# RWKV-7 and pooling trunk on one core: the value turned by VectorE through DRAM, the key norm's reciprocal spread through DRAM, scalings, bonus and gate moved

## The chip, the cores and the metric

The kernel runs on one core of a Trainium2 chip. The metric is the device time of one execution in microseconds (us). The engines are called as the profile calls them: PE is TensorE (matmuls and transposes by matmul), DVE is VectorE, ACT is ScalarE, POOL is GpSimd, SP is SyncE, which here only issues DMAs; SPq and ACTq are the queues of DMAs that SP and ACT issue.

## What is computed

One layer of a decoder trunk on 512 tokens of width 2048, all in float32, then an RMSNorm. Cut to what matters here:

```python
z = rms_norm(x) @ W_in            # r, k, v, decay and rate inputs | gate | pool input | pool gate
zs = zs + (token_shift(zs) - zs) * mu
w = exp(-exp(-softplus(-(w0 + tanh(wd) @ w_up)) - 0.5)); a = sigmoid(a0 + ad @ a_up)
kk = k * k_k;  kk = kk / max(norm(kk over each head's 64 channels), 1e-12)
k = k * (1 + (a - 1) * k_a)
# per head (16 heads of 64), token after token:
S = S * w + (S @ -kk) (kk * a)^T + v k^T;   y = S @ r
y = head_group_norm(y) * ln_w + ln_b
y_rwkv = (y + sum(r * k * r_k) * v) * silu(g_rwkv)
# pool half: trailing means over 2, 4, 8, 16 tokens, a 256x256 map per group, times silu(gate)
x = x + concat(y_rwkv, y_pool) @ W_out
x = x + sigmoid(x @ W_pg + b_pg) * (p @ W_ple);   out = rms_norm(x) * final_g
```

## The kernel before

Everything lies with channels on the partitions and the 512 tokens along the free axis. Large products are made of three matmuls (`mm3`, L164): each operand is split into a rounded high part and the rest, and high by high, high by low and low by high are summed in PSUM. A weight chunk (128 rows by 512, or four 128x128 tiles side by side) is loaded raw by a DMA on SP, cast to its high part by ACT (L132), and its low part is a subtraction on DVE (L133). The pool of chunks has four buffers of each kind, so chunk n takes the buffers of chunk n-4: its raw load waits for the subtraction of chunk n-4 on DVE, and its cast for the last matmul that uses chunk n-4. The raw loads are queued on SP in the order of the chunks, among SP's other DMAs. Engines execute in order, and the order on each engine is fixed when the program is built: a scheduler places the instructions, except that the order of PE's matmuls is held as the program issues them (`keep_in_program_order`, L156), and that `tc.issue_after(i)` keeps an instruction behind instruction i.

The 16 heads are worked in eight blocks j of two heads (128 channels). A block goes through these functions:

- `prepare_key` (L554): kk is the square of the scaled key (ACT), split into high `kqh` (ACT) and low `kql` (DVE, L138).
- `norm_key` (L563): PE sums the squares of each head, `pss`; DVE evicts it with a maximum (L568). `scale_key` (L570): DVE's reciprocal over 128x512 (L572) and a product (L573). (The reciprocal is taken of the sum of squares; the root isn't needed, as kk enters twice.)
- `decay_and_rate` (L519): two small products `pu` and `pa`, the tile `sig` and its running sum, the decays `pw` and `ipw`, the rate `tha`.
- `prepare` (L577): on DVE the operands `ar` (L594, L597) and `bk` (L596, and its second half L600, which needs the scaled key kk and tha), and `kp`; SP stores bk to DRAM (L607).
- `scores` (L617): 32 matmuls `pm` from bk and ar, masked into `mt` on DVE (L632); `pbo` and the bonus `bv`; then mt's small blocks go through DRAM (nd, L648, and n, L653), and bk comes back as `bg` in pieces of 32x32x32 (L659) for two DVE block transposes into `bkn` (L614).
- `invert` (L664): 31 steps on DVE invert the small triangular blocks; the result goes through DRAM (xd, L679) into `x1` (L686), four reads on SP.
- `gather` (L692): the next block's `prepare_key` and `decay_and_rate`; the value `v_` is turned by four PE transposes into `pv` (L702) and copied by ACT into `uv` (L704, L705); the next block's `norm_key`; y1, two 32x256 block transposes of x1 on DVE (L729); 32 matmuls each `pq` (from y1), `pmv` and `px`. Then the pending `finish` of the block before.
- `recur` (L762): eight chunks of 64 tokens, one after the other: py, zs, pu, uv, ps and sbd go round PE, DVE and ACT. At its end the eight statistics of y and the eight scalings of `ysb` (L866).
- `finish` (L870): PE transposes ysb into `pyt` (L874), ACT adds the norm's bias, DVE adds the bonus and multiplies with the gate (L877, L878), and ACT's queue stores the result.

Each engine's share of this is filled with the large projections: `pump(n)` lets PE go on with n matmuls of the streams zk, zr, zv, zg and zb (the next block's key, receptance, value and gate, and a pooling unit's columns). The counts are constants (L517, L883), so PE's place in the stream at each step of a block is the same every time the program is built. In the loop at L901 a turn prepares block j+1 (`prepare`), runs the recurrence of block j with `scores(j+1)` and `invert(j+1)` woven in, and ends with `gather(j+1)`. After the eight blocks come the output product acc_o and the embedding gate acc_g, with weights streamed in the same way. The gather of block j is called gather(j) here: it works for block j and begins block j+1.

Of the kernel before, what the change touches and what calls it, by code (L numbers as in the profile page):

```python
# [34 lines left out]
def trunk_kernel(ctx: ExitStack, tc: tile.TileContext, x, p, norm_g, w_in, mu, w0, w_up, a0, a_up,  # L35
# [527 lines left out]
    def norm_key(j):  # L563
# [4 lines left out]
        late[0] = nc.vector.tensor_scalar(kk, ps, 1e-24, None, ALU.max)  # L568

    def scale_key(j):  # L570
        k_, kk = need("k", j), kks[j][0]
        nc.vector.reciprocal(kk, kk)  # L572
# [4 lines left out]
    def prepare(j):  # L577
# [22 lines left out]
        nc.vector.tensor_tensor(bk[:, :, 1:3, :], k4, i4, ALU.mult)  # L600
# [16 lines left out]
    def scores(j):  # L617
# [43 lines left out]
        st_[j].update(mt=mt, nb=nb, bv=bv, bg=bg)


    def invert(j):  # L664
# [18 lines left out]
        for par in range(2):  # L683
            pb = 64 * (1 - par)
            for b in range(2):
                nc.sync.dma_start(out=x1[pb + 32 * b:pb + 32 * b + 32, :, 32 * b:32 * b + 32],  # L686
                                  in_=xd[par, b].rearrange("u i q c -> (i q) u c"))
# [4 lines left out]
    def gather(j):  # L692
        d = st_[j]
        v_, mt = d.pop("v_"), d["mt"]
        if j + 1 < NJ:
# [32 lines left out]
        with tc.issue_after(late[0].ins):  # L728
            yt = [nc.vector.transpose(y1[pb:pb + 32], x1[pb:pb + 32, :, 0:32]) for pb in (0, 64)]  # L729
# [464 lines left out]
```

## Time and profile before

| | us |
|---|---|
| median of three runs | 1085.88 (1085.88, 1084.61, 1088.7) |
| the profiled execution | 1087.06 |
| its span | 1085.3 |
| busy: PE | 1057.8 |
| busy: DVE | 714.9 |
| busy: ACT | 441.3 |
| busy: POOL | 70.9 |
| mean granted clock of TensorE | 0.996 |

The profiled execution was 1.2 us above the median and 1.8 us longer than its span, which runs from the first to the last recorded instruction. The eight blocks take the first 720 us of the span or so, acc_o and acc_g the rest. A row of the timeline gives start and duration in us, engine, line, operation, output and inputs, the shape, and in brackets how long the engine had waited and for what. Durations on PE are those of the whole pipeline: the next matmul can start before the one ahead of it has ended, so PE's pace is read from one start to the next. On DVE, too, the next instruction starts some 0.07 us before the recorded end of the last.

### The profile page before, as it was taken

The page shows a single profiled execution, that of the slowest core. Times are in us where ns is not written, and L with a number is a line of the kernel's source. Part 1 is how long each engine was busy: PE and PEld are TensorE (multiplying, and loading weights), DVE is VectorE, ACT ScalarE, POOL GpSimd, SP SyncE. Part 2 cuts the span into 40 slices and gives each one's busy share as a digit, 9 for nine tenths or more (in the row PEclk, how much of TensorE's full clock was granted, in tenths as well). Part 3 has the DMA queues.
Part 4 walks back from the last instruction along what each step waited for, and adds up shares of the span by engine and source line. Part 5 has one row for each costly group of instructions (what it writes and reads, how often), then busy time and mean ns, then how long its engine had stood idle before and what let it go on. Part 6 is the DMA issues. An engine that isn't in the chain of part 4 may idle for free.

```text
span 1085.3 us, 17105 instructions
## 1 busy us (share of the span) xinstructions
PE 1057.8 (97%) x5996; PEld 873.7 (80%) x5996; DVE 714.9 (66%) x1851; ACT 441.3 (41%) x901; POOL 70.9 (7%) x180
## 2 busy tenths in 40 slices
PE   5999999999999999999999999999999999999996
PEld 4888878888888887887888788888888888888885
DVE  6676968878779779688887966464432424445366
ACT  7633535335336244353353344543222222333337
POOL 2100010010110100100101101000000000000000
PEclk9999999999999999999999999999999999999999
DMA  7444443442533533433435343774434428354534
GB/s 234 112 120 113 135 115 86 114 123 74 156 93 110 143 95 100 117 87 107 115 95 152 99 127 104 244 238 152 166 126 142 168 97 263 129 180 150 178 99 156
DMA packets 212916, 146.94 MB, mean 135 GB/s; under 512 B 68085, under 2 KB 173150, under 8 KB 212830
## 3 DMA queue, kind: packets, MB, share of 16 engines
q1 hardware_dynamic: 192126, 112.28, 35.9%
q10 hardware_dynamic: 20704, 33.56, 9.5%
q8 instruction: 47, 0.77, 0.3%
q14 instruction: 39, 0.32, 0.1%
HBM read 122.21 MB, written 23.07 MB: 134 GB/s over the span
## 4 chain that ended last, share of the span: by engine, by line
PE 76%; DVE 4%; DMA 1%; ACT 1%; issue 0%; SPq 0%; ACTq 0%; DVEq 0%
PE acc_o L157 16%; PE acc_g L157 16%; PE zb L157 13%; PE zg L157 5%; PE zv L157 5%; PE zr L157 5%; PE zk L157 4%; PE pple L157 2%; PE py L157 2%; PE pu L157 1%; PE pm L157 1%; DMA n<-nd 1%; PE pp L157 1%; PE ps L157 1%; PE pmv L157 1%; PE px L1015 1%
## 5 line engine op out<-in xcount | busy, mean ns | idle before, releaser
L133 DVE TENSOR_TENSOR wlo_g<-raw_g,whi_g 128x512 fp32r<-128x512 f32 x84 | 57.1, 685 | 76.0 <-ACT whi_g L132 76.0
L157 PE MATMUL zb<-hhi,whi_b 128*128 128x512 f32 x256 | 106.0, 414 | 0.0
L133 DVE TENSOR_TENSOR wlo_o<-raw_o,whi_o 128x512 fp32r<-128x512 f32 x64 | 43.9, 690 | 91.4 <-ACT whi_o L132 91.4
L157 PE MATMUL zb<-hhi,wlo_b 128*128 128x512 f32 x256 | 100.4, 392 | 0.0
L157 PE MATMUL acc_o<-whi_o,ylo 128*128 128x512 f32 x256 | 100.2, 391 | 0.0
L157 PE MATMUL acc_o<-whi_o,yhi 128*128 128x512 f32 x256 | 99.9, 390 | 0.0
L157 PE MATMUL zb<-hlo,whi_b 128*128 128x512 f32 x256 | 99.8, 390 | 0.0
L157 PE MATMUL acc_o<-wlo_o,yhi 128*128 128x512 f32 x256 | 99.7, 390 | 0.0
L132 ACT CAST whi_g<-raw_g 128x512 fp32r<-128x512 f32 x84 | 52.0, 621 | 106.4 <-PE acc_g L157 59.4
L157 PE MATMUL acc_g<-whi_g,x2hi 128*128 128x512 f32 x208 | 81.2, 391 | 0.0
L157 PE MATMUL acc_g<-wlo_g,x2hi 128*128 128x512 f32 x208 | 81.0, 389 | 0.0
L157 PE MATMUL acc_g<-whi_g,x2lo 128*128 128x512 f32 x208 | 80.6, 389 | 0.0
L132 ACT CAST whi_o<-raw_o 128x512 fp32r<-128x512 f32 x64 | 39.9, 623 | 97.0 <-PE acc_o L157 96.7
L827 POOL TENSOR_SCALAR s0p<-sbd,pw 64x64 f32<-64x64 f32 x96 | 54.5, 568 | 338.6 <-DVE sbd L820 251.0
L132 ACT CAST whi_b<-raw_b 128x512 fp32r<-128x512 f32 x64 | 39.7, 621 | 85.4 <-PE zb L157 28.8
L133 DVE TENSOR_TENSOR wlo_b<-raw_b,whi_b 128x512 fp32r<-128x512 f32 x64 | 43.7, 684 | 28.0 <-ACT whi_b L132 27.6
L157 PEld LDWEIGHTS zb<-hhi,wlo_b 128*128 128x128 f32 x256 | 48.0, 188 | 10.9
L675 DVE TENSOR_TENSOR xw<-xw,tm 128x60 f32<-128x60 f32 (+24 forms) x248 | 52.1, 210 | 7.0
L157 PEld LDWEIGHTS acc_o<-wlo_o,yhi 128*128 128x128 f32 x256 | 48.1, 188 | 10.0
L157 PEld LDWEIGHTS acc_o<-whi_o,ylo 128*128 128x128 f32 x256 | 48.1, 188 | 9.8
L157 PEld LDWEIGHTS acc_o<-whi_o,yhi 128*128 128x128 f32 x256 | 48.1, 188 | 9.7
L157 PEld LDWEIGHTS zb<-hhi,whi_b 128*128 128x128 f32 x256 | 48.2, 188 | 8.3
(283 smaller groups left out, 2532.0 us busy)
## 6 DMA issues: line engine op xcount, KB each, us to landing
raw_b<-in_w_in_dram SPq DMA_DIRECT2D x64, 256.0 KB
raw_o<-in_w_out_dram SPq DMA_DIRECT2D x64, 256.0 KB
raw_g<-in_w_pg_dram SPq DMA_DIRECT2D x64, 256.0 KB
raw_k<-in_w_in_dram SPq DMA_DIRECT2D x32, 256.0 KB
raw_r<-in_w_in_dram SPq DMA_DIRECT2D x32, 256.0 KB
raw_v<-in_w_in_dram SPq DMA_DIRECT2D x32, 256.0 KB
raw_g<-in_w_in_dram SPq DMA_DIRECT2D x32, 256.0 KB
bkd<-bk SPq DMA_DIRECT2D x8, 512.0 KB
```

The costliest lines, as they stand in the source:

```text
L132: nc.scalar.copy(hi, raw)
L133: nc.vector.tensor_tensor(lo, raw, hi.bitcast(F32), ALU.subtract)
L157: i = nc.tensor.matmul(*a, **k)
L675: nc.vector.tensor_tensor(xw[:, 0:n_, s + 1:32], xw[:, 0:n_, s + 1:32], tm[:, 0:n_, 0:w_], ALU.add)
L827: nc.gpsimd.tensor_scalar(s0p[hc, :], nxt[hc, hc], pcn[hc], None, ALU.mult)
L1015: nc.tensor.transpose(pt[:, tt * P:(tt + 1) * P], x2[tt][:, i * P:(i + 1) * P], ident)
```

## The change

It has four parts.

The value. The four PE transposes and two ACT copies go. In `prepare` SP stores `sv` to DRAM (vd, 256 KB, behind the last x1 read); after the n reads in `scores` four DMAs on SP fetch it back as `vg` in pieces of 32x16x32, and in `gather` two DVE block transposes of 64x512 make uv from it. vg takes one of the four buffers of the tag "t"; in `gather` the next block's sig takes that buffer again, so that ACT's write of sig waits for the two transposes.

The key's norm. `prepare_key(j+2)` and `norm_key(j+2)` are called at the fifth and sixth chunk of `recur(j)`; they were called in `gather(j+1)`. For all blocks but block 0, ACT evicts pss, one row of each head (2x512) goes to DRAM (nrd), comes back as 128x8 (nr), the maximum and the reciprocal run on 128x8, and the result goes to DRAM (ird) and comes back as kk in two broadcast reads of 64x512, all on SP. Block 1's key keeps its place in gather(0).

The scalings of ysb move from the end of `recur` into the next `gather`, behind the two y1 transposes. The bonus and the gate of `finish` (two DVE instructions, one DMA on ACT's queue) move into the next block's `prepare`, behind the second half of bk.

What stands on PE otherwise is the same sequence, with the 32 transposes pv gone and each pss of blocks 2 to 7 some chunks earlier. SP issues 75 DMAs more in all (607 for 532): five for each value, and five for each key's norm from block 1 on. In the first gather, gather(0), the rows on DVE around the y1 transposes were these (names carry the block's number: y10 is the y1 of block 0, kk1 the key of block 1):

```order
L133 TENSOR_TENSOR wlo_b0_1_1059<-raw_b0_1_1056,whi_b0_1_1058 128x512
L592 TENSOR_TENSOR kp1_1646<-kp1_1646,sk1_1280 128x512
L568 TENSOR_SCALAR kk1_1429<-pss1_1489 128x512
L729 STREAM_TRANSPOSE y10_1548<-x10_1150 32x256 x2
L572 RECIPROCAL kk1_1429<-kk1_1429 128x512
L133 TENSOR_TENSOR wlo_b0_2_1065<-raw_b0_2_1062,whi_b0_2_1064 128x512
L133 TENSOR_TENSOR wlo_b0_3_1159<-raw_b0_3_1156,whi_b0_3_1158 128x512
L370 SCALAR_TENSOR_TENSOR sv1_1523<-zv1_1383,prm_131,sv1_1523 128x511
```

and are now:

```order
L609 TENSOR_TENSOR kp1_1657<-kp1_1657,sk1_1287 128x512
L610 TENSOR_SCALAR tha1_1463<-tha1_1463 128x512
L611 TENSOR_TENSOR ar1_1655<-sr1_1387,pw1_1455 128x4x2x64
L613 TENSOR_TENSOR bk1_1656<-kp1_1657,ipw1_1456 128x4x2x64
L614 SCALAR_TENSOR_TENSOR ar1_1655<-sk1_1287,dprm_133,pw1_1455 128x4x128
L133 TENSOR_TENSOR wlo_b0_2_1072<-raw_b0_2_1069,whi_b0_2_1071 128x512
L526 TENSOR_TENSOR as2_1654<-ar2_1651,as2_1654 64x128
L758 STREAM_TRANSPOSE y10_1560<-x10_1157 32x256
L133 TENSOR_TENSOR wlo_b0_3_1166<-raw_b0_3_1163,whi_b0_3_1165 128x512
L370 SCALAR_TENSOR_TENSOR sv1_1535<-zv1_1390,prm_131,sv1_1535 128x511
L758 STREAM_TRANSPOSE y10_1560<-x10_1157 32x256
```

The second y10 transpose stands behind two products into ar, one into bk, two weight subtractions and the shift of the value sv1, and the reciprocal is gone. On SP, in the same gather, the reads of x10 stood here:

```order
L129 DMA raw_b0_2_1062<-in_w_in_dram 128x4x128
L679 DMA xd0_1145<-xw0_1080 256x1x32 x2
L129 DMA raw_b0_3_1156<-in_w_in_dram 128x4x128
L686 DMA x10_1150<-xd0_1145 32x8x32 x4
L129 DMA raw_g1_0_1162<-in_w_in_dram 128x4x128
L129 DMA raw_g1_1_1184<-in_w_in_dram 128x4x128
```

and stand here now:

```order
L129 DMA raw_b0_2_1069<-in_w_in_dram 128x4x128
L708 DMA xd0_1152<-xw0_1087 256x1x32 x4
L129 DMA raw_b0_3_1163<-in_w_in_dram 128x4x128
L129 DMA raw_g1_0_1169<-in_w_in_dram 128x4x128
L129 DMA raw_g1_1_1191<-in_w_in_dram 128x4x128
L715 DMA x10_1157<-xd0_1152 32x8x32 x4
L129 DMA raw_g1_2_1197<-in_w_in_dram 128x4x128
```

The weight loads g1_0 and g1_1 are ahead of x10's reads. A little later, ahead of block 1's pm, DVE had these rows up to the second half of bk (L600, in the changed kernel L617):

```order
L597 SCALAR_TENSOR_TENSOR ar1_1644<-sk1_1280,dprm_133,pw1_1448 128x4x128
L599 TENSOR_TENSOR kk1_1429<-kk1_1429,tha1_1456 128x512
L133 TENSOR_TENSOR wlo_g1_0_1165<-raw_g1_0_1162,whi_g1_0_1164 128x512
L600 TENSOR_TENSOR bk1_1645<-kk1_1429,ipw1_1449 128x4x128
L601 SCALAR_TENSOR_TENSOR kp1_1646<-sr1_1380,dprm_133,kp1_1646 128x512
L526 TENSOR_TENSOR as2_1643<-ar2_1640,as2_1643 64x128
L133 TENSOR_TENSOR wlo_g1_1_1187<-raw_g1_1_1184,whi_g1_1_1186 128x512
```

and has now:

```order
L133 TENSOR_TENSOR wlo_g1_1_1194<-raw_g1_1_1191,whi_g1_1_1193 128x512
L851 TENSOR_SCALAR sbd1_567<-ps0_0_1703,pw0_837 64x64 x2
L133 TENSOR_TENSOR wlo_g1_2_1200<-raw_g1_2_1197,whi_g1_2_1199 128x512
L590 SCALAR_TENSOR_TENSOR kk1_1436<-sk1_1287,prm_131,kk1_1436 128x512
L616 TENSOR_TENSOR kk1_1436<-kk1_1436,tha1_1463 128x512
L133 TENSOR_TENSOR wlo_g1_3_1218<-raw_g1_3_1215,whi_g1_3_1217 128x512
L617 TENSOR_TENSOR bk1_1656<-kk1_1436,ipw1_1456 128x4x128
```

Where one weight subtraction of g1 stood ahead of bk's second half, all four stand now, the last directly ahead of it. In gather(4), where block 3's ysb is scaled, DVE had from the second y1 transpose on:

```order
L729 STREAM_TRANSPOSE y14_5274<-x14_5081 32x256
L151 SCALAR_TENSOR_TENSOR rs83_5159<-nt83_5162,rs83_5159 128x8
L596 TENSOR_TENSOR bk5_5369<-kp5_5370,ipw5_5202 128x4x2x64
L866 TENSOR_SCALAR ysb3_4554<-ysb3_4554,mvr3_5142,rs83_5159 128x64 x2
L133 TENSOR_TENSOR wlo_g5_3_2906<-raw_g5_3_2903,whi_g5_3_2905 128x512
L866 TENSOR_SCALAR ysb3_4554<-ysb3_4554,mvr3_5142,rs83_5159 128x64 x6
L417 TENSOR_TENSOR sw4_1_5249<-u4_5247 128x511
L418 COPY sw4_1_5249<-u4_5247 128x1
L572 RECIPROCAL kk5_5182<-kk5_5182 128x512
```

and has now:

```order
L418 COPY sw4_1_5297<-u4_5295 128x1
L614 SCALAR_TENSOR_TENSOR ar5_5420<-sk5_4884,dprm_133,pw5_5252 128x4x128
L417 TENSOR_TENSOR sw4_2_5300<-sw4_1_5297 128x510
L418 COPY sw4_2_5300<-sw4_1_5297 128x2
L133 TENSOR_TENSOR wlo_k6_0_2941<-raw_k6_0_2938,whi_k6_0_2940 128x512
L420 TENSOR_TENSOR sw4_2_5300<-sw4_2_5300,rc1_505 128x4
L903 TENSOR_SCALAR ysb3_4601<-ysb3_4601,mvr3_5207,rs83_5224 128x64
L421 SCALAR_TENSOR_TENSOR u4_5295<-sw4_2_5300,u4_5295 128x512
L903 TENSOR_SCALAR ysb3_4601<-ysb3_4601,mvr3_5207,rs83_5224 128x64 x4
L138 TENSOR_TENSOR dl1_5306<-u4_5295,dh1_5305 128x512
L903 TENSOR_SCALAR ysb3_4601<-ysb3_4601,mvr3_5207,rs83_5224 128x64 x3
L590 SCALAR_TENSOR_TENSOR kk5_5014<-sk5_4884,prm_131,kk5_5014 128x512
```

The reciprocal over 128x512 is gone from behind the scalings, and a pooling unit's sums (sw4, u4, dl1) and a product into ar stand between them and the transpose. The core of the diff:

```diff
+        if j == 0:
+            nc.vector.tensor_scalar(kk, ps, 1e-24, None, ALU.max)
+            nc.vector.reciprocal(kk, kk)
+            return
+        nc.scalar.copy(kk, ps)
+        nrd = dram.tile([2, T], F32, name=f"nrd{j}", tag="nrd")
+        nc.sync.dma_start(out=nrd, in_=kk[0::64, :])
+        nr = rw.tile([P, 8], F32, name=f"nr{j}", tag="nr")
+        nc.sync.dma_start(out=nr, in_=nrd.rearrange("h (p e) -> (h p) e", e=8))
+        nrs[j] = nr
+
+    def spread_norm(j):
+        nr, kk = nrs.pop(j), kks[j][0]
+        nc.vector.tensor_scalar(nr, nr, 1e-24, None, ALU.max)
+        nc.vector.reciprocal(nr, nr)
+        ird = dram.tile([2, T], F32, name=f"ird{j}", tag="ird")
+        nc.sync.dma_start(out=ird.rearrange("h (p e) -> (h p) e", e=8), in_=nr)
+        for h in range(2):
+            nc.sync.dma_start(out=kk[64 * h:64 * h + 64], in_=ird[h:h + 1].to_broadcast([64, T]))
 
     def scale_key(j):
         k_, kk = need("k", j), kks[j][0]
-        nc.vector.reciprocal(kk, kk)
         nc.vector.scalar_tensor_tensor(kk, k_, pc("k_k", j), kk, ALU.mult, ALU.mult)
         kks[j] = kk
...
+        made = nc.vector.tensor_tensor(bk[:, :, 1:3, :], k4, i4, ALU.mult)
+        with tc.issue_after(made.ins):
+            nc.vector.scalar_tensor_tensor(kp, r_, dp(49, j), kp, ALU.mult, ALU.mult)
+            if gates:
+                gates.pop()()
         kph = rw.tile([P, T], F32R, name=f"kph{j}", tag="t", bufs=4)
         kpl = rw.tile([P, T], F32R, name=f"kpl{j}", tag="t", bufs=4)
         split(kph, kpl, kp)
 
+        vd = dram.tile([P, T], F32, name=f"vd{j}", tag="vd")
+        with tc.issue_after(read[-1].ins) if read else ExitStack():
+            nc.sync.dma_start(out=vd, in_=v_)
         bkd = dram.tile([P, NCH * P], F32, name=f"bkd{j}", tag="bkd")
         nc.sync.dma_start(out=bkd, in_=bk.rearrange("p q s c -> p (q s c)"))
-        st_[j] = dict(pw=pw, ar=ar, bk=bk, bkd=bkd, v_=v_, kp=(kph, kpl))
+        st_[j] = dict(pw=pw, ar=ar, bk=bk, bkd=bkd, vd=vd, v_=v_, kp=(kph, kpl),
+                      vg=rw.tile([P, NT, 4, 32], F32, name=f"vg{j}", tag="t", bufs=4))
...
+        vg = st_[j]["vg"]
+        with tc.issue_after(n_.ins):
+            for q in range(4):
+                nc.sync.dma_start(out=vg[32 * q:32 * q + 32],
+                                  in_=st_[j]["vd"].rearrange("(b k) (c q i) -> q k c b i", b=4, q=4, i=32)[q])
...
-                nc.sync.dma_start(out=x1[pb + 32 * b:pb + 32 * b + 32, :, 32 * b:32 * b + 32],
-                                  in_=xd[par, b].rearrange("u i q c -> (i q) u c"))
+                read.append(nc.sync.dma_start(out=x1[pb + 32 * b:pb + 32 * b + 32, :, 32 * b:32 * b + 32],
+                                              in_=xd[par, b].rearrange("u i q c -> (i q) u c")))
...
-        v_, mt = d.pop("v_"), d["mt"]
+        mt = d["mt"]
         if j + 1 < NJ:
-            prepare_key(j + 1)
+            if j == 0:
+                prepare_key(1)
             decay_and_rate(j + 1)
 
         uv = rw.tile([P, NCH, P], F32, name=f"uv{j}", tag="uv")
-        ps = psY.tile([P, T], F32, name=f"pv{j}", tag="y")
-        for tt in range(NT):
-            tr(ps[:, tt * P:(tt + 1) * P], v_[:, tt * P:(tt + 1) * P], ident)
-        pv = ps.rearrange("p (t c) -> p t c", c=P)
-        nc.scalar.copy(uv[0:64, 0::2, :], pv[0:64])
-        nc.scalar.copy(uv[64:128, 1::2, :], pv[64:128])
-
+        vg = d.pop("vg")
+        for h in range(2):
+            hr = slice(64 * h, 64 * h + 64)
+            nc.vector.transpose(uv[hr, h::2, :].rearrange("p c (b k) -> p c b k", k=32), vg[hr])
...
+        if j == 0:
+            norm_key(1)
         if j + 1 < NJ:
-            norm_key(j + 1)
+            with tc.issue_after(read[-1].ins):
+                spread_norm(j + 1)
...
-        with tc.issue_after(late[0].ins):
-            yt = [nc.vector.transpose(y1[pb:pb + 32], x1[pb:pb + 32, :, 0:32]) for pb in (0, 64)]
-        if j + 1 < NJ:
-            with tc.issue_after(yt[0].ins), tc.issue_after(yt[1].ins), tc.issue_after((normed or yt)[-1].ins):
+        yt = [nc.vector.transpose(y1[pb:pb + 32], x1[pb:pb + 32, :, 0:32]) for pb in (0, 64)]
+        with tc.issue_after(yt[0].ins), tc.issue_after(yt[1].ins):
+            if normed:
+                normed.pop()()
+            if j + 1 < NJ:
                 scale_key(j + 1)
...
         if pending:
-            pending.pop()()
+            gates.append(pending.pop()())
...
             pump(HC2)
+            if j + 2 < NJ and ch == 5:
+                norm_key(j + 2)
...
             step()
+            if j + 2 < NJ and ch == 4:
+                prepare_key(j + 2)
...
+        def scale():
+            for i in range(8):
+                last = nc.vector.tensor_scalar(y8[:, i, :], y8[:, i, :], mvr[:, i, 0:1], rs8[:, i, :],
+                                               ALU.subtract, ALU.mult)
+            return last
+
+        if j + 1 < NJ:
+            normed.append(scale)
+        else:
+            scale()
...
-            nc.vector.tensor_tensor(yo, yo, bv, ALU.add)
-            nc.vector.tensor_tensor(yo, yo, sg, ALU.mult)
-            nc.scalar.dma_start(out=yd[j], in_=yo)
+
+            def gate_out():
+                nc.vector.tensor_tensor(yo, yo, bv, ALU.add)
+                nc.vector.tensor_tensor(yo, yo, sg, ALU.mult)
+                nc.scalar.dma_start(out=yd[j], in_=yo)
+
+            return gate_out
```

More of the change, by code (lines that the diff above doesn't have):

```diff
@@ L513, in need @@
         return zt[nm, j]
-    pws, kks, late = {}, {}, [None]
+    pws, kks, nrs, read = {}, {}, {}, []
     H1, H2, H3, H4, H5, HE = 6, 12, 20, 8, 13, 40
@@ L567, in norm_key @@
         mm(ps, blk, kql, start=False, stop=True)
-        late[0] = nc.vector.tensor_scalar(kk, ps, 1e-24, None, ALU.max)
+        if j == 0:
[16 more added lines that the diff above has]
+            nc.sync.dma_start(out=kk[64 * h:64 * h + 64], in_=ird[h:h + 1].to_broadcast([64, T]))
     def scale_key(j):
         k_, kk = need("k", j), kks[j][0]
-        nc.vector.reciprocal(kk, kk)
         nc.vector.scalar_tensor_tensor(kk, k_, pc("k_k", j), kk, ALU.mult, ALU.mult)
@@ L599, in prepare @@
         nc.vector.tensor_tensor(kk, kk, tha, ALU.mult)
-        nc.vector.tensor_tensor(bk[:, :, 1:3, :], k4, i4, ALU.mult)
-        nc.vector.scalar_tensor_tensor(kp, r_, dp(49, j), kp, ALU.mult, ALU.mult)
+        made = nc.vector.tensor_tensor(bk[:, :, 1:3, :], k4, i4, ALU.mult)
[3 more added lines that the diff above has]
+                gates.pop()()
         kph = rw.tile([P, T], F32R, name=f"kph{j}", tag="t", bufs=4)
@@ L864, in recur @@
         rsqrt(rs8, ve8, nt8)
-        for i in range(8):
-            last = nc.vector.tensor_scalar(y8[:, i, :], y8[:, i, :], mvr[:, i, 0:1], rs8[:, i, :],
-                                           ALU.subtract, ALU.mult)
-        normed.append(last)
+        def scale():
[7 more added lines that the diff above has]
+            scale()
         def finish():
@@ L885, in trunk_kernel @@
     HP = 1000
-    pending, normed = [], []
+    pending, normed, gates = [], [], []
     need("k", 0)
@@ L914, in trunk_kernel @@
             prepare(j + 1)
+        elif gates:
+            gates.pop()()
         recur(j, invert(j + 1) if j + 1 < NJ else iter(()), between)
@@ L918, in trunk_kernel @@
     pump(HE)
-    pending.pop()()
+    pending.pop()()()
     s2a.close()
```

## The prediction

> **What bounds the kernel now.** I read the page first: PE is busy in nearly the whole span, and the chain that ended last runs over PE.
>
> ```profile
> PE 1057.8 (97%) x5996; PEld 873.7 (80%) x5996; DVE 714.9 (66%) x1851; ACT 441.3 (41%) x901; POOL 70.9 (7%) x180
> PE 76%; DVE 4%; DMA 1%; ACT 1%; issue 0%; SPq 0%; ACTq 0%; DVEq 0%
> ```
>
> So time can only be won by taking work off PE or by shortening PE's waits, and it is lost wherever PE waits anew; DVE's 66% matters only where a result is late for PE. PE's waits are few. These are the ones inside the blocks that this change can touch (in all, how often, longest):
>
> ```profile
> PE pm L157 <- DVE bk L600: 3.1, 2, 2.0
> PE pq L157 <- DVE y L729: 1.7, 2, 0.8
> PE pu L157 <- DVE zs L794: 0.7, 2, 0.4
> ```
>
> PE's timeline has them one by one, beside a pm that didn't wait (353.27):
>
> ```profile
> 194.13 0.69 PE L157 MATMUL pq<-y,mt 32*32 32x32 f32 x30 [0.82 <-DVE y L729]
> ...
> 353.27 2.06 PE L157 MATMUL pm<-ar,bk 64*128 64x128 f32 x32
> ...
> 427.70 3.01 PE L157 MATMUL pm<-ar,bk 64*128 64x128 f32 x32 [2.04 <-DVE bk L600]
> ...
> 489.43 0.69 PE L157 MATMUL pq<-y,mt 32*32 32x32 f32 x30 [0.83 <-DVE y L729]
> ...
> 502.94 2.06 PE L157 MATMUL pm<-ar,bk 64*128 64x128 f32 x32 [1.09 <-DVE bk L600]
> ```
>
> The pm at 427.70 also takes 1 us longer. The table of windows says why: the granted clock (0.50, the last column but two) was halved behind that wait.
>
> ```profile
> 428.60:432.00 3.40, 3.40 (x25) 2.98 (x22) 3.02 (x7) 0.00 (x0) 0.00 (x0) 0.50 0.69 232
> ```
>
> Half a clock for 3.4 us is 1.7 us lost, so this one wait cost 2.04 + 1.7 = 3.7 us. Waits of 1.09, 0.83 and 0.82 us were followed by no such window.
>
> **What leaves PE.** The value's transposes:
>
> ```profile
> L161 PE MATMUL pv<-ident,sv 128*128 128x128 f32 x32 | 4.8, 272 | 0.0
> ...
> 257.28 0.60 PE L161 MATMUL pv<-ident,sv 128*128 128x128 f32 x4
> 257.63 0.47 PE L157 MATMUL zb<-hhi,whi_b 128*128 128x512 f32 x1
> 257.95 0.39 PE L157 MATMUL zb<-hlo,whi_b 128*128 128x512 f32 x1
> ```
>
> The group's 4.8 us is pipelined time. By starts, pv and the matmul behind it take 257.28 to 257.95, 0.67 us, where a matmul of the stream takes 0.23 (0.39 a row, the next starting 0.23 on): 0.44 us for each block, eight times, is **3.5 us** won. They lie on PE with nothing to hide them, so this is sure. The pss matmuls only change place.
>
> **What leaves DVE ahead of bk.** In blocks 2 to 7 the second half of bk now has less ahead of it:
>
> ```profile
> L572 DVE RECIPROCAL kk<-kk 128x512 f32<-128x512 f32 x8 | 26.7, 3334 | 0.0
> L568 DVE TENSOR_SCALAR kk<-pss 128x512 f32<-128x512 f32 x8 | 5.5, 684 | 0.0
> L878 DVE TENSOR_TENSOR yo<-yo,sg 128x512 f32<-128x512 f32 x8 | 5.5, 685 | 0.1
> L877 DVE TENSOR_TENSOR yo<-yo,bv 128x512 f32<-128x512 f32 x8 | 5.5, 684 | 0.8 <-ACT yo L876 0.8
> L614 DVE STREAM_TRANSPOSE bkn<-bg 128x512 f32<-128x512 f32 x16 | 10.9, 696 | 0.0
> L866 DVE TENSOR_SCALAR ysb<-ysb,mvr,rs 128x64 f32<-128x64 f32 x64 | 15.6, 307 | 0.1
> ```
>
> Gone from there: 3.33 + 0.68 + 0.68 + 0.68 = 5.4 us. Added: two block transposes for uv, at 0.70 each by their twin bkn (half the partitions, as many elements on each), 1.4, and a maximum and a reciprocal on 128x8, small. bk comes some 4 us earlier, and the waits of 2.04 and 1.09 both go, with the half clock: 3.7 + 1.1 = **4.8 us**. Next latest there is kk's return from DRAM. One trip, from the last write of xd to the first read of x1, took 403.45 - 400.87 = 2.6 us:
>
> ```profile
> 400.87 0.56 SPq L679 DMA_DIRECT2D xd<-xw  x1
> 403.45 0.33 SPq L686 DMA_DIRECT2D x<-xd  x1
> ```
>
> The write of ird stands behind the x1 reads, at about 406.5, so kk is back at about 412, ahead of the scalings that stand before it on DVE: covered. With the maximum gone from ahead of y1, the wait of 0.82 at 194 goes (**0.8 us**); in gather(5), where the statistics of ysb still stand ahead, I keep the 0.83. Won in all: 3.5 + 4.8 + 0.8 = 9.1 us.
>
> **New wait A: pq in the first gather.** Block 1's key is still made there. In the order, y10's second transpose now stands behind work of `prepare(1)` that followed it before, and uv's transposes are ahead of sig:
>
> ```profile
> 111.26 0.74 DVE L370 SCALAR_TENSOR_TENSOR sr<-zr,prm,sr 128x511 f32<-128x511 f32 x1
> ...
> 113.41 1.23 DVE L534 TENSOR_TENSOR_SCAN sig<-seg,sig 128x512 f32<-128x512 f32 x1
> 114.55 0.53 DVE L591 TENSOR_SCALAR kp<-tha,dprm 128x512 f32<-128x512 f32 x1
> 114.99 0.69 DVE L133 TENSOR_TENSOR wlo_b<-raw_b,whi_b 128x512 fp32r<-128x512 f32 x1
> 115.59 0.69 DVE L592 TENSOR_TENSOR kp<-kp,sk 128x512 f32<-128x512 f32 x1
> ...
> 116.81 0.90 DVE L729 STREAM_TRANSPOSE y<-x 32x256 f32<-32x256 f32 x2
> ...
> 122.15 0.74 DVE L370 SCALAR_TENSOR_TENSOR sv<-zv,prm,sv 128x511 f32<-128x511 f32 x1
> ...
> 120.53 0.69 PE L157 MATMUL pq<-y,mt 32*32 32x32 f32 x32
> ```
>
> A full tile takes 0.6 us from start to start (114.99 to 115.59), kp's first 0.44. From kp to the end of y10 DVE now does kp 0.44, eight full tiles (wlo, kp, tha, ar, bk, ar, wlo, wlo) at 0.6, as 0.2, sv 0.7 and y 0.9: 7.0 us. If kp begins at 114.55 as before, y10 is done at 121.5; if the transposes (two at 0.65) and ACT's sig behind them push it back by all of 1.5, at 123.1. pq is due at 120.53 less 0.44. The wait is 1.4 to 3.0; I take **2.8**, since sig can't start before the transposes end. x10's reads, now behind the load g1_1, are back by 120 or so and don't set it.
>
> **New wait B: pm of block 1.** The last of g1's weight subtractions now stands directly ahead of bk's second half. Its cast takes the buffer that the stream's last matmul before pm reads:
>
> ```profile
> 132.37 0.62 ACT L132 CAST whi_g<-raw_g 128x512 fp32r<-128x512 f32 x1 [1.80 <-PE zb L157]
> ...
> 133.02 0.69 DVE L133 TENSOR_TENSOR wlo_g<-raw_g,whi_g 128x512 fp32r<-128x512 f32 x1 [1.73 <-ACT whi_g L132]
> ...
> 132.45 2.06 PE L157 MATMUL pm<-ar,bk 64*128 64x128 f32 x32
> ```
>
> Before, pm at 132.45 didn't need that subtraction. Now bk can begin only at 133.02 + 0.6, and pm 0.7 later, at 134.4: **1.9 us**. This holds whatever DVE did before.
>
> **New wait C: pyt in gather(4).** The scalings now end behind a pooling unit's sums:
>
> ```profile
> 410.86 0.43 DVE L729 STREAM_TRANSPOSE y<-x 32x256 f32<-32x256 f32 x1
> ...
> 417.02 0.60 PE L161 MATMUL pyt<-ident,ysb 128*128 128x128 f32 x4
> ```
>
> pyt is due 0.9 earlier than 417.02 (0.44 of pv, 0.46 of two pss matmuls), 416.1. From y1's end on DVE there stand eight full tiles at 0.6, eight scalings at 0.25 (15.6 us by 64) and eight small ones at 0.08, 7.5 us; y1's end, at 411.3 before, comes some 0.9 to 1.2 earlier without the maximum and its small neighbours ahead of it, so ysb is ready at 417.6 to 417.9: a wait of 1.5 to 1.8; I take **1.5**. In the other gathers no pooling sums stand there, and the scalings come in time, with as little as nothing to spare in gather(5).
>
> The rest costs nothing while its cover holds: 75 more DMAs on SP delay weight loads that lie chunks ahead, and ACT's copy of pss takes the place of two copies of pv.
>
> **The sum.** Won 9.1, lost 2.8 + 1.9 + 1.5 = 6.2: 2.9 us faster with the clock untouched. But A and B are as long as the wait of 2.04 that halved the clock, and each may cost 1.7 more. I take one such window: 2.9 - 1.7 = 1.2 us faster. The profiled execution was at 1087.06, so the changed kernel would be at 1085.9; it lay 1.2 above the median, so **1084.7 us**.
>
> [...]
>
> **The rivals.**
>
> 1. Neither A nor B halves the clock: 2.9 us faster, 1083.0. Against it speaks the window behind 2.04 us; for it, that this is a single case. [...]
> 2. The early waits aren't there, or the rows that I set one behind the other overlap: only C remains, 9.1 - 1.5 = 7.6 us faster, 1078.3. For it speaks that 4 us of relief on DVE in six blocks may carry further than the listed waits; against it that B follows from the order alone. It decides in favour of "faster" once A, B and the clock together come to under 2.2 us.
> 3. Slower: the norm's row comes back late. The maximum on nr stands inside the recurrence, just before the last zs, with all of DVE behind it; PE would wait as in the third row of its waits.
>
> ```profile
> 390.37 0.69 DVE L133 TENSOR_TENSOR wlo_b<-raw_b,whi_b 128x512 fp32r<-128x512 f32 x1
> ...
> 394.82 0.18 DVE L671 TENSOR_TENSOR tm<-xw,n 128x24 f32<-128x24 f32 x1
> ...
> 396.26 0.28 DVE L794 TENSOR_TENSOR zs<-py,mv 64x128 f32<-64x128 f32 x1 [0.61 <-PE py L157]
> ```
>
> On SP the read of nr stands behind a weight load that waits for the subtraction at 390.37, so it is issued at about 391.4 and lands, by one trip, at 394.0; its use on DVE comes with the row at 394.82, and zs has 0.6 to spare. It decides from some 2.5 us of lateness. Coming 4 us later than I place it, it would cost 1.3 us or so in each of seven blocks, 9 us: 1093.8. For it speaks that 10 more DMAs share SP's queue in each block; against it that bkn, fed by four reads in small pieces (its idle time above is 0.0), never waited. [...]
>
> **How the numbers follow.** One half-clock window 0.36, none 0.13, both 0.14, the early waits absent 0.25, the norm late 0.12. 0.5% is 5.4 us, about what a measurement of this kernel can tell from no change: faster means under 1080.5, slower over 1091.3. Faster is the case of the absent waits with a little of the case of no window, 0.27; slower is most of the norm's case, 0.10; the same, 0.63. For the range I leave out the slow case and the best of the absent waits (all 9.1 won is 1076.8): 1077 to 1090.5.
>
> **What would show it.** Right: pq of the first gather waits 1.4 to 3 us for y, pm of block 1 about 1.9 for bk, pyt near 417 for ysb; no pm of blocks 5 and 6 waits; the clock falls behind A or B. Wrong: PE's waits inside the blocks come to less than 2 us in all, or zs waits for nr, block after block.

## The result and the profile after

The changed kernel is slower: 1095.07 us in the median of six runs (1092.81 to 1099.53), against 1085.29 for the kernel before (six runs, 1084.14 to 1088.7). The ratio is 1.0089 [1.0074, 1.0104], 9.8 us. The forecast was 1084.7 with a range up to 1090.5.

The profiled execution took 1099.53, the longest of the six, with a span of 1097.8. Here are the page's busy times, the shares of the chain, and the row of the cores (span and mean granted clock):

```profile
PE 1060.8 (97%) x5964; PEld 875.7 (80%) x5964; DVE 701.2 (64%) x1867; ACT 435.0 (40%) x892; POOL 74.8 (7%) x180
PE 77%; DVE 5%; DMA 3%; issue 2%; ACT 1%; SPq 0%; ACTq 0%; DVEq 0%
core 0: 1097.8 us, clock 0.989
```

DVE's work fell by 13.7 us and PE issues 32 matmuls fewer, as meant; yet PE is busy longer, and the clock was at 0.996 before. What the chain calls DVE, DMA and issue has grown: PE waits more, and it runs more of the time at half speed. Its waits inside the blocks (in all, how often, longest):

```profile
PE px L157 <- issue: 4.1, 3, 2.3
PE pq L157 <- DVE y L758: 4.0, 2, 2.2
PE py L157 <- DVE sbd L853: 3.8, 3, 1.4
...
PE pm L157 <- DVE bk L617: 2.2, 1, 2.2
...
PE pyt L161 <- DVE ysb L903: 0.7, 1, 0.7
PE pq L157 <- DVE sw L420: 0.6, 1, 0.6
PE pu L157 <- DVE zs L825: 0.2, 1, 0.2
```

px is new; pq waited 1.7 before and py 0.8. The pm waits of blocks 5 and 6 are gone; the pm that is left is block 1's. PE's timeline has them one by one:

```profile
121.68 0.21 PE L157 MATMUL pq<-y,mt 32*32 32x32 f32 x2 [1.81 <-DVE y L758]
124.05 0.69 PE L157 MATMUL pq<-y,mt 32*32 32x32 f32 x30 [2.16 <-DVE y L758]
...
141.31 0.38 PE L157 MATMUL pm<-ar,bk 64*128 64x128 f32 x2 [2.24 <-DVE bk L617]
...
205.75 0.69 PE L157 MATMUL px<-x,q 32*32 32x32 f32 x32 [1.10 <-issue]
...
355.17 0.69 PE L157 MATMUL px<-x,q 32*32 32x32 f32 x32 [2.25 <-issue]
```

Behind each of these four places the clock is halved. The table of windows (the last column but two is the granted clock):

```profile
124.60:131.40 6.80, 6.80 (x81) 5.80 (x75) 0.98 (x3) 2.92 (x7) 0.40 (x1) 0.51 0.23 72
141.80:145.20 3.40, 3.40 (x30) 3.08 (x28) 3.32 (x8) 0.62 (x1) 0.00 (x0) 0.50 0.67 235
206.60:210.00 3.40, 3.40 (x11) 2.75 (x11) 3.09 (x6) 0.62 (x3) 0.55 (x1) 0.51 0.34 99
356.80:360.20 3.40, 3.40 (x10) 2.50 (x9) 2.79 (x5) 1.70 (x3) 0.00 (x0) 0.51 0.68 234
```

That is 17.0 us at half speed, 8.5 us lost, where the execution before lost 1.7.

Every timed run has its span and granted clock, so this holds for the medians too. Span times (1 - clock) is what a run lost to the clock, span times clock is the rest. The clock is given to three digits, so each value is good to some 0.5 us. Part of each loss costs nothing: all twelve profiled executions end in a half-speed stretch that begins after PE's last matmul (with the change that matmul starts at 1088.5 and the clock falls at 1090.7; before, 1076.3 and 1080.5). Up to the end of the span this stretch counts 1.8 to 3.6 us as lost, so two rows of the table can differ by nearly 2 us for it alone. In the six runs the clock was 0.989 to 0.991. The table has the medians over the runs of each kernel (the experiments are told below), and of the runs of before that were timed beside it on the same chip (the change itself has no clocks of before beside it; in its row stand those of e1 to e4 and of e5 to e8):

| kernel | median us | ratio to before | lost to the clock: before, this | rest: before, this |
|---|---|---|---|---|
| the change | 1095.07 | 1.0089 [1.0074, 1.0104] | 3.3 to 4.3, 10.4 | 1081.3 to 1082.6, 1082.9 |
| e1_abload | 1088.77 | 1.0023 [1.0011, 1.0034] | 3.3, 7.6 | 1081.3, 1079.8 |
| e2_first | 1088.94 | 1.0023 [1.0009, 1.0037] | 3.3, 6.0 | 1081.3, 1080.9 |
| e3_novalue | 1088.33 | 1.0016 [1.0007, 1.0025] | 3.3, 6.5 | 1081.3, 1080.4 |
| e4_valueonly | 1100.18 | 1.0131 [1.0111, 1.0151] | 3.3, 11.5 | 1081.3, 1086.5 |
| e5_both | 1082.51 | 0.9952 [0.9936, 0.9968] | 4.3, 2.7 | 1082.6, 1077.5 |
| e6_novalue_abload | 1089.67 | 1.0008 [0.9993, 1.0023] | 4.3, 4.4 | 1082.6, 1083.3 |
| e7_both_scaled | 1085.39 | 0.9973 [0.9956, 0.9989] | 4.3, 5.4 | 1082.6, 1077.6 |
| e8_both_gated | 1081.72 | 0.9944 [0.9924, 0.9964] | 4.3, 3.2 | 1082.6, 1076.8 |
| e9_novalue_both | 1083.09 | 0.9976 [0.9966, 0.9986] | 4.3, 3.2 | 1080.5, 1078.8 |
| e10_scale_first | 1078.59 | 0.9930 [0.9917, 0.9943] | 4.3, 2.2 | 1080.5, 1074.7 |

Of the 9.8 us, then, some 6 to 7 are the clock. The profiled pair agrees: 8.5 less 1.7 is 6.8, without the stretch at the end. In the medians the waits outweigh what was won by some 2 us or less; in the profiled pair, whose changed run is the longest of its six, 12.5 - 6.8 = 5.7 us are left for them.

**Where the waits come from.** DVE's timeline in the first gather has the two y10 transposes and what stood between them:

```profile
121.10 0.43 DVE L758 STREAM_TRANSPOSE y<-x 32x256 f32<-32x256 f32 x1
...
122.31 0.69 DVE L133 TENSOR_TENSOR wlo_b<-raw_b,whi_b 128x512 fp32r<-128x512 f32 x1 [0.77 <-ACT whi_b L132]
...
123.58 0.42 DVE L758 STREAM_TRANSPOSE y<-x 32x256 f32<-32x256 f32 x1
```

Both come late, one behind the other, with a wait of 0.77 for a weight's cast on ACT in between; the first two of pq's matmuls need only the first transpose, hence the two waits. Ahead of block 1's pm DVE shows:

```profile
138.57 0.75 DVE L590 SCALAR_TENSOR_TENSOR kk<-sk,prm,kk 128x512 f32<-128x512 f32 x1 [1.05 <-DMA kk<-ird]
139.36 0.69 DVE L616 TENSOR_TENSOR kk<-kk,tha 128x512 f32<-128x512 f32 x1
139.97 0.69 DVE L133 TENSOR_TENSOR wlo_g<-raw_g,whi_g 128x512 fp32r<-128x512 f32 x1
140.57 0.68 DVE L617 TENSOR_TENSOR bk<-kk,ipw 128x512 f32<-128x512 f32 x1
```

The weight subtraction stands directly ahead of bk, as forecast; but DVE first waited 1.05 for the norm's row to come back from DRAM, and that set the last of the delay: the subtraction's cast on ACT was done at 139.50, so that without kk it could have begun 0.5 earlier.

The px waits were not foreseen. DVE, ACT's queue and ACT in gather(1) and, in the last three rows, gather(3):

```profile
203.90 0.29 DVE L526 TENSOR_TENSOR us<-ur,us 64x128 fp32r<-64x128 f32 x1
204.26 0.47 ACTq L354 DMA_DIRECT2D ur<-in_w_up_dram  x1
204.91 0.36 ACT L772 COPY q<-pq 32x256 f32<-32x256 f32 x1 [1.49 <-DVE ysb L903]
...
352.02 0.29 DVE L526 TENSOR_TENSOR us<-ur,us 64x128 fp32r<-64x128 f32 x1
352.38 1.77 ACTq L354 DMA_DIRECT2D ur<-in_w_up_dram  x2
354.33 0.74 ACT L772 COPY q<-pq 32x256 f32<-32x256 f32 x2 [4.68 <-DMA raw_k<-in_w_in_dram]
```

px needs the copies q of pq (L772), which ACT makes. pq began at 202.88, and q needs nothing from DVE. But ACT also issues the load of ur, the raw weights of a later block's decay (`load_ab`, L354), and the scheduler had set that load directly in front of q, a whole turn of the loop ahead of its place in the program. ur has one buffer: the load waits until DVE's `us` (L526) has read the one before. The load follows `us` by 0.07 us in both places, and q follows the load. (The releasers that the profile names for q, ysb and raw_k, can't be it: neither is an input of q or holds its buffer.) In the order on ACT, the first piece of the load stands ahead of q in gather(1); it stood ahead of q there before the change, too:

```order
L354 DMA ur4_3571<-in_w_up_dram 64x128
L772 COPY q21_2537<-pq21_2520 32x256 x2
L354 DMA ur4_3571<-in_w_up_dram 64x128
```

On DVE, `us3` stood well ahead of both y1 transposes of this gather before the change; now it stands behind both, after a product into bk and one into ar:

```order
L758 STREAM_TRANSPOSE y11_2508<-x11_2287 32x256
L133 TENSOR_TENSOR wlo_g2_0_1424<-raw_g2_0_1421,whi_g2_0_1423 128x512
L149 TENSOR_TENSOR nt80_2388<-rs80_2385,ve80_2386 128x8
L613 TENSOR_TENSOR bk2_2619<-kp2_2620,ipw2_2414 128x4x2x64
L150 TENSOR_TENSOR nt80_2388<-nt80_2388,rs80_2385 128x8
L614 SCALAR_TENSOR_TENSOR ar2_2618<-sk2_2088,dprm_133,pw2_2413 128x4x128
L151 SCALAR_TENSOR_TENSOR rs80_2385<-nt80_2388,rs80_2385 128x8
L526 TENSOR_TENSOR us3_2613<-ur3_2610,us3_2613 64x128
```

The load that was harmless in front of q is now held by an instruction that DVE reaches after pq.

The py waits are in blocks 3, 5 and 7, early in the inversion. DVE's first step waits for the small blocks n to come back from DRAM, and sbd, which py needs, stands behind the first steps. The rows of block 3 after the change:

```profile
305.73 0.19 DVE L700 TENSOR_TENSOR tm<-i,n 128x31 f32<-128x31 f32 x1 [3.51 <-DMA n<-nd]
...
308.01 0.28 DVE L853 SCALAR_TENSOR_TENSOR sbd<-ps,pw,s0p 64x64 f32<-64x64 f32 x1
...
309.26 0.49 PE L157 MATMUL py<-sbd,ar 128*128 128x128 f32 x2 [1.39 <-DVE sbd L853]
```

and before:

```profile
293.61 0.19 DVE L671 TENSOR_TENSOR tm<-i,n 128x31 f32<-128x31 f32 x1 [2.53 <-DMA n<-nd]
...
297.15 0.49 PE L157 MATMUL py<-sbd,ar 128*128 128x128 f32 x2 [0.41 <-DVE sbd L820]
```

DVE waits 3.51 for n where it waited 2.53, and py waits 1.39 for 0.41: the same 0.98.

### The profile page after: what moved, and what is told of

Read it like the earlier page. It is cut to its first block, busy times and chain, and to the rows that moved or that the text cites. A ratio compares the mean times of both kernels' runs of the same rounds, so it can differ in the third digit from the quotient of the medians.

```text
span 1097.8 us, 17172 instructions
## 1 busy us (share of the span) xinstructions
PE 1060.8 (97%) x5964; PEld 875.7 (80%) x5964; DVE 701.2 (64%) x1867; ACT 435.0 (40%) x892; POOL 74.8 (7%) x180
## 4 chain that ended last, share of the span: by engine, by line
PE 77%; DVE 5%; DMA 3%; issue 2%; ACT 1%; SPq 0%; ACTq 0%; DVEq 0%
PE acc_o L157 16%; PE acc_g L157 16%; PE zb L157 12%; PE zv L157 6%; PE zr L157 6%; PE zg L157 5%; PE zk L157 4%; DMA n<-nd 2%; PE py L157 2%; PE pple L157 2%; PE pu L157 1%; PE pm L157 1%; PE pp L157 1%; PE ps L157 1%; PE pmv L157 1%
```

## The experiments

The theory after the result: four separate waits, each with its own cause (A and B in the first gather, C, and the load on ACT's queue), and a half clock that comes with most of them. The rival: it is the value's traffic as such, through DVE's transposes or SP's queue, and the named waits are its symptoms. The medians and intervals are those of the table above. Kernels that were timed on different chips have different runs of before beside them, whose medians were 1085.3 to 1088.5, so they are compared by their ratios; 0.1% is 1.1 us.

**e1_abload: the load held behind q.** The changed kernel, with ACT's load issued after the last q copy of the gather.

```diff
-            load_ab(j + 1)
+            with tc.issue_after(lastq[0].ins) if lastq[0] else ExitStack():
+                load_ab(j + 1)
...
-                nc.scalar.copy(q2t[pb + 32:pb + 64], ps3[pb + 32:pb + 64])
+                lastq[0] = nc.scalar.copy(q2t[pb + 32:pb + 64], ps3[pb + 32:pb + 64])
```

> The changed kernel with one constraint more: the loads of the decay and rate weights (ur, ar) on ACT's queue are kept behind the two copies of q of the gather before them. Theory 'stalls' (the loss is a handful of PE waits, each with its cause in an engine's order, and half a clock behind the longest): in the changed kernel ACT stands at the load of ur, which waits for DVE's subtraction us, and the copies of q stand behind it, so px waits 1.1, 0.7 and 2.3 us in gathers 1 to 3; all three go, and the half clock behind two of them, some 3 us: 7 us less than the changed kernel, about 1088. Rival 'traffic' (75 more DMAs and their trips through DRAM delay everything a little): px waits because q is late anyway, under 1 us less, 1094 to 1095.

The ratio fell from 1.0089 to 1.0023, by 7.2 us. No px row is left among PE's waits. The others are still there, and two of them are shorter as well (pq 2.6 for 4.0, py 1.7 for 3.8):

```profile
PE pq L157 <- DVE y L759: 2.6, 2, 1.4
PE pm L157 <- DVE bk L618: 2.3, 1, 2.3
PE py L157 <- DVE sbd L854: 1.7, 3, 0.8
```

So the load's place on ACT is shown to be the cause of the px waits. The 7.2 us are the worth of the whole edit, the shorter pq and py among them. By the table some 3 us of it are the clock's (10.4 to 7.6) and some 3 the rest's (1082.9 to 1079.8).

**e2_first: A and B undone.** Block 1's norm stays on DVE as before the change, `prepare(1)` goes behind both y10 transposes, and the raw loads of g1 go behind x10's reads.

```diff
-        if j == 0:
+        if j <= 1:
             nc.vector.tensor_scalar(kk, ps, 1e-24, None, ALU.max)
-            nc.vector.reciprocal(kk, kk)
+            if j == 0:
+                nc.vector.reciprocal(kk, kk)
             return
...
         k_, kk = need("k", j), kks[j][0]
+        if j == 1:
+            nc.vector.reciprocal(kk, kk)
...
-            prepare(j + 1)
+            with tc.issue_after(y0[0].ins) if j == 0 else ExitStack(), tc.issue_after(y0[1].ins) if j == 0 else ExitStack():
+                prepare(j + 1)
```

> The changed kernel with the first block put right: block 1's key norm is taken on DVE over 128x512 as before, not through DRAM; block 1's prepare is kept behind both y10 transposes, and the weight loads g1 on SP behind x10's reads. Theory 'stalls': the waits of pq in the first gather (4.2 us in all) and of pm in block 1 (2.3) go, and with them both half-clock windows of about 1.6 each: 9.7 us less, about 1085.5. Rival 'traffic': only five DMAs less, so 1 us less at most; the two waits come back elsewhere, 1094.

1.0023 again, 7.2 us faster than the change and less than expected. The pm wait is gone, pq keeps 1.3 of its 4.0, px 3.5 of its 4.1, and py has 4.4 for 3.8:

```profile
PE py L158 <- DVE sbd L860: 4.4, 3, 1.5
PE px L158 <- issue: 3.5, 3, 1.7
...
PE pq L158 <- DVE y L763: 1.3, 1, 1.3
```

What is left at pq has another cause: the second transpose still stands behind the shift of sv1. Which of the three parts of this edit does how much wasn't taken apart.

**e5_both: e1 and e2 together.**

> Both repairs on the changed kernel: the ur and ar loads behind the copies of q, and the first block put right. If the loss is the sum of separate waits, the gains add up: 6.3 and 6.2 us off 1095, about 1082.5, with a pq wait near 1 us in the first gather, pyt's in gather 4 and py's for sbd left, and no half clock. If the two repairs took away the same thing (the half clock of one window, say), about 1086.

0.9952 [0.9936, 0.9968]: 1.37% or 14.9 us faster than the change, where e1 and e2 won 7.2 each. They add up; the two causes are separate. The value's traffic is all there in this kernel, and of the norm's only block 1's share is gone, so traffic as such isn't what made the change slow. PE's waits in the blocks are down to these and two of 0.4 and 0.3, and the clock of the profiled execution is 0.998:

```profile
PE py L158 <- DVE sbd L861: 1.7, 4, 0.7
PE pq L158 <- DVE y L764: 1.0, 1, 1.0
...
PE pyt L162 <- DVE ysb L911: 0.7, 1, 0.7
PE pq L158 <- DVE sw L421: 0.4, 1, 0.4
```

With its two new causes of waiting mended, the change is faster than before by 0.5%.

**e3_novalue: the change with the value on PE as before.** pv and its copies are back, vd and vg gone.

> The changed kernel with the value turned on PE as before (no vd, no vg, 40 DMAs less); norm, scalings, bonus and gate as in the changed kernel. Theory 'stalls': the order by itself puts y10's transposes and bk's second half of block 1 early again, so both early waits and their half clocks go (9.7), pv comes back (3.5), the px wait of gather 2 goes: some 6.5 us less than the changed kernel, 1088.5. Theory 'traffic': more than half of the extra DMAs go, so half of the loss: 1090, and above all the waits of py for sbd in blocks 3, 5 and 7 (n lands 1 us later than before) go back to their old 0.2 to 0.4.

1088.33, a ratio of 1.0016. The size was as expected, for a different reason than expected: neither pq nor pm waits any more, so in this kernel the value's route (the transposes into uv and the order that they bring) is needed for A and B. But px waits 3.6 in the first gather. Here it is the load of ar and DVE's `as`:

```profile
122.14 0.27 DVE L526 TENSOR_TENSOR as<-ar,as 64x128 fp32r<-64x128 f32 x1
...
122.49 0.47 ACTq L354 DMA_DIRECT2D ar<-in_a_up_dram  x1
...
124.23 0.74 ACT L765 COPY q<-pq 32x256 f32<-32x256 f32 x2
...
125.07 1.06 PE L157 MATMUL px<-x,q 32*32 32x32 f32 x32 [3.57 <-issue]
```

The same chain with the other load: pq had run at 119.74.

**e6_novalue_abload: e3 with e1's edit.**

> All of the change but the value (which is turned on PE as before), with the ur and ar loads behind the copies of q. Against the run without the value the px wait of 3.6 us in the first gather goes, and the two half-clock windows behind it (3.4): 1081.5. This and the run with both repairs say whether the value's turn by VectorE pays at all once the waits are gone: if its 3.5 us of PE count, the run with both repairs is the faster of the two by up to 3.5; if its DVE and DMA work takes that back, this one is.

1089.67, a ratio of 1.0008, and a miss: the px of 3.6 was expected to go and the time with it. It fell to 0.9, but the new order of DVE brought block 1's pm back, 2.3, now with DVE waiting 5.17 for kk from DRAM:

```profile
131.80 0.75 DVE L590 SCALAR_TENSOR_TENSOR kk<-sk,prm,kk 128x512 f32<-128x512 f32 x1 [5.17 <-DMA kk<-ird]
```

So B has two causes of its own, the subtraction and the norm's return, and the value isn't needed for the second. Also, py waits 3.8 in five places here, and px 1.2 in gather(5) behind another thing that ACT does ahead of q, the cast of `dh` that waits for DVE's u. An edit that frees one instruction moves the order elsewhere.

**e9_novalue_both: e5 with the value on PE.** What the value's route is worth once A, B and the load are mended.

> All of the change but the value, with both repairs (ur and ar loads behind the copies of q; block 1's norm on DVE, its prepare behind y10, g1 behind x10's reads). It differs from the run with both repairs in the value's turn alone. Theory 'PE counts': without stalls PE sets the time, so pv's 0.44 us in each block come back, 3.5 us; pq's wait of 1.2 in the first gather goes, and px of gather 5 waits 1.2 behind a pooling unit's cast on ACT, which stands ahead of q: 0.4% more than the run with both repairs, ratio to before 0.999. Rival 'the turn on DVE costs what it saves': as fast or faster, 0.995 or less.

1083.09, 0.9976 [0.9966, 0.9986], where e5 had 0.9952 [0.9936, 0.9968]: by this the value's route is worth 0.24%, 2.6 us, of the 3.5 forecast. The two intervals meet at their ends, so the size is good to some 2 us. It is also the difference of two whole kernels: e9 has waits that e5 hasn't, a px of 1.2 in gather(5) with half clock behind it and a pu of 1.1.

**e4_valueonly: before, with the value's route alone.**

> The kernel before with the value alone turned by VectorE through DRAM; key norm, scalings, bonus and gate as before. Theory 'stalls': 3.5 us of PE won; y10's transposes stand behind the value's shift, so pq of the first gather waits 2 to 3 us with half a clock behind (1.6), px of gather 1 waits about 1; the old waits of pm in blocks 5 and 6 stay: 1086 to 1088. Theory 'traffic': the 40 DMAs delay n, py waits 1 us more in blocks 3, 5, 7, and little else: 1085.

1100.18, a ratio of 1.0131 [1.0111, 1.0151]: the slowest of all, and a miss. The waits are those of before, much longer:

```profile
PE pm L157 <- DVE bk L600: 6.9, 3, 3.4
...
PE pq L157 <- DVE y L736: 5.0, 2, 3.8
```

In before, the pm waits of blocks 5 and 6 were 2.04 and 1.09; with 1.4 us of block transposes more on DVE ahead of bk, and PE earlier by pv's 0.44, each is 3.4. That covers the 1.3 that the first grew by, and not all of the 2.3 of the second; the rest wasn't traced. And pq and pm run slow behind their waits, the half clock again (a mean granted clock of 0.68 from 124 to 140 us, 0.69 from 436 to 441 and 0.66 from 513 to 518):

```profile
124.24 1.43 PE L157 MATMUL pq<-y,mt 32*32 32x32 f32 x32 [3.77 <-DVE y L736]
...
437.00 3.00 PE L157 MATMUL pm<-ar,bk 64*128 64x128 f32 x32 [3.35 <-DVE bk L600]
...
513.34 3.50 PE L157 MATMUL pm<-ar,bk 64*128 64x128 f32 x32 [3.36 <-DVE bk L600]
```

So without the relief of DVE that the other parts bring, the value's turn costs 14 us.

**e7_both_scaled and e8_both_gated: e5 without one of the moves.** e7 has the scalings of ysb back at the end of `recur`, e8 has the bonus and the gate back in `finish`.

```diff
-        if j + 1 < NJ:
-            normed.append(scale)
-        else:
-            scale()
+        scale()
```

> Both repairs, and the scalings of ysb back at the end of the recurrence, ahead of the y1 transposes where the order puts them. Theory: pyt's wait of 1.3 us in gather 4 goes, pq's wait for y1 in gathers 2 and 5 (0.8 each before the change) comes back or grows: within 1.5 us of the run with both repairs. If the scalings' move is what shortens the handover, 3 us or more slower.

> Both repairs, and the bonus and gate back in the gather, ahead of bk. Theory: bk has some 4 us to spare in blocks 2 to 7, so 1.4 us more ahead of it cost nothing: the same as the run with both repairs within 1 us. Rival (the value's two transposes eat the spare, as the run with the value alone showed with pm waits of 3.4): pm waits for bk in blocks 5 and 6, 2 us or more slower.

Both were timed beside e5 (1082.51) and the same runs of before. e7 took 1085.39, 2.9 us more, though the intervals overlap; e8 took 1081.72, the same. In e7 the pyt wait is gone, and pq waits 2.25 in gather(5), where the scalings now stand ahead of it again:

```profile
484.10 1.05 PE L158 MATMUL pq<-y,mt 32*32 32x32 f32 x30 [2.25 <-DVE sw L421]
```

By the table the rest of e7 is e5's (1077.6 and 1077.5), and the whole difference is the clock (5.4 and 2.7): several small waits were traded for one of 2.2, at no price in waits and 2.7 in clock. e7's own runs show how much this varies from run to run: 1082.65 us at a clock of 0.998, 1090.92 at 0.990, and 0.008 of 1085 is 8.7 us, about the difference of 8.3.

**e10_scale_first: e5 with the scalings given priority in `gather`.** The remaining forecast wait, C, taken out.

```diff
             if normed:
-                normed.pop()()
+                with tc.high_priority(offset=HP):
+                    normed.pop()()
```

> The run with both repairs, and the deferred scalings of ysb at high priority, so that in gather 4 they stand ahead of the second half of the pooling unit's sums on DVE, some 2 us earlier. Theory: pyt's wait for ysb in gather 4 (1.2 us by starts) goes and nothing else moves: ratio to before 0.994. Rival: the pooling unit's sums, now later, hold ACT's cast of dh and with it q or weight casts, and the wait moves: 0.995 to 0.997.

1078.59 for 1086.31, a ratio of 0.9930 [0.9917, 0.9943]: 7.7 us faster than before, and the best version; it beats both kernels. Over e5 that is 0.2%, with intervals that overlap. pyt comes in time, four in a row and without a wait:

```profile
414.05 0.60 PE L162 MATMUL pyt<-ident,ysb 128*128 128x128 f32 x4
```

## Why the prediction was wrong, point by point

**What leaves PE (3.5).** Right in kind. e9 against e5 gives 2.6 for the whole route, its costs on DVE among it.

**What leaves DVE ahead of bk (4.8).** Right: no pm of blocks 5 and 6 waits after the change. That DVE's work ahead of bk sets these waits, is shown from the other side by e4, where they grow to 3.4. The 0.8 of pq at 194 went too, and the one in gather(5) stayed with 0.64.

**Wait A (2.8).** Right in place and cause, mis-sized: 4.0. The working had DVE's instructions back to back; the 0.77 for the cast on ACT wasn't in it, and kp itself began at 116.35 for 114.55. The upper bound of 3.0 was made of the delay by uv's transposes alone.

**Wait B (1.9).** Right in place, 2.24. The step "This holds whatever DVE did before" was too narrow: a second late arrival, kk's return from DRAM, set the last half microsecond. The forecast had covered kk's return for blocks 2 to 7, by the scalings ahead of it, and not looked at block 1.

**Wait C (1.5).** Right in place; two of the four transposes waited 0.72, and PE lost 1.3 by starts. e10 takes it out.

**"The rest costs nothing while its cover holds: 75 more DMAs on SP [...], and ACT's copy of pss takes the place of two copies of pv."** This step failed. It counted what the change adds to SP and ACT, and not what stands on ACT already that waits for a DVE instruction which the change moves. The px waits, 4.1 us and two half-clock windows, came of that; e1 shows it.

**"I take one such window."** This step failed by most. Each of the four places was followed by half clock, one for two windows: 17 us at half speed for the 3.4 taken. The single case of before, 2.04 us, had been used as a price that might fall due once; it is a price on nearly every wait of that size (the last section has them), and two of the four were px's, which the forecast hadn't at all. Over the runs the clock made up some 6 to 7 of the 9.8 us.

**The rivals.** The third had the sign and nearly the size (1093.8), and not the mechanism: PE waited for zs 0.2 in all, less than the 0.7 before, and DVE for nr 0.6, once. The norm's way back held PE in block 1 alone; in block 3 DVE waited 0.57 for it, at no cost to PE. The first is out, as both A and B were followed by half clock (6.83 and 3.41 us); 1.7 us lost behind each, and nothing more, makes 1086.4 by the forecast's terms. The second is out.

**The sum made again**, for the profiled execution against that of before: won 9.1; lost, by starts on PE, 4.2 (A), 2.3 (B), 1.3 (C), 4.2 (px), 3.0 (py beyond before's) and 8.5 of clock: 14.4 slower, where the measured difference is 1099.53 - 1087.06 = 12.5. The 8.5 counts the windows as if PE had been busy throughout, and a wait beside a window is partly counted twice; I can't place the 1.9 more closely.

**What stays open.** Why n comes back later in blocks 3, 5 and 7. From the issue of its reads to the first step it took 6.59, 6.42 and 6.34 us before, and 7.58, 7.39 and 7.37 after. Neither of two suspicions holds: e6 has it (7.60, 7.40, 6.85) without the value's DMAs and e4 doesn't (6.14, 6.63, 6.19) with them, and e3 doesn't (6.71, 6.10, 6.02) with all of the norm's. It cost some 3 us here; in e5 it is mostly gone (6.70, 6.55, 6.10). Of e5's two halves e1 takes most of it (6.44, 6.93, 6.97) and e2 none (7.58, 7.69, 7.62), but e6 has e1's edit too, and I have no edit that moves it alone.

## What to carry to other kernels

Where a change moves instructions on one engine, list for each of them who waits for it, buffers included, and then what stands *behind that waiter* on its own in-order queue: here a DMA issue on ScalarE, far ahead of its use, held two copies that PE needed. Price a PE wait of two microseconds or more as the wait and a window of half clock: eleven of the twelve here had one behind them. Between one and two it was four of twenty-four, so several small waits came cheaper than one long wait of the same sum. And take the parts of a combined change apart before judging one of them: the value's turn alone cost 14 us, inside the mended whole it earned about 2.6.

## What the runs showed of the hardware

**The half clock.** In the records of the granted clock every half-speed stretch but the last, which is cut off by the end, is 3.41, 6.83 or 10.24 us, and the four of the change's profiled execution begin whole multiples of 3.413 us apart (124.7, 141.8, 206.6, 356.8: 5, 19 and 44 such steps). This table has, over the profiled executions, PE's waits inside the blocks of 1.0 us and more, by the idle time in the timeline's brackets, and the half-speed time that goes with each. It begins between 0.6 us ahead of the wait's end and 1.9 behind it.

| wait, us | half speed, us | kernel |
|---|---|---|
| 4.0 (1.81 and 2.16) | 6.83 | the change, pq |
| 3.77 | 10.24 | e4, pq |
| 3.57 | 6.83 | e3, px |
| 3.35, 3.36 | 3.41, 3.41 | e4, pm |
| 2.6 (1.19 and 1.42) | 6.83 | e1, pq |
| 2.32 | 3.41 | e6, pm |
| 2.30 | none | e1, pm |
| 2.25 | 6.83 | e7, pq |
| 2.25 | 3.41 | the change, px |
| 2.24 | 3.41 | the change, pm |
| 2.04 | 3.41 | before, pm |
| 1.66, 1.10 | 3.41, 3.41 | e2, px |
| 1.17 | 3.41 | e9, px |
| 1.10 | 3.41 | the change, px |
| 1.17 | none | e6, px |
| 1.00 to 1.56, nineteen waits | none | several, none of them px |

Of the waits of 2 us or more only one was not followed by it, e1's pm of 2.30, and below 1.0 none was; between, length doesn't decide: 1.10 was followed and 1.56 wasn't, 1.17 was in e9 and wasn't in e6. All four below 2 us that were followed are px's, which stand between the small matmuls of pmv (64x64) and px itself (32x32). What decides between 1 and 2 us, and what makes the clock of e7's runs differ, no run here shows.

**A queue that computes and loads.** A load's issue on ACT held back the copies behind it for as long as its buffer was in use (it began 0.07 us after DVE's `us` had read it, and px waited 1.10 and 2.25), and each piece took 0.47 us or more of ACT's queue after that (352.38, two pieces in 1.77).
